# Split weights in the delta rule's own tiles, and no GpSimd splits at stage ends, in a two-block fp32 transformer

## The chip, the cores and the metric

The kernel runs on one core of one Trainium2 chip. The metric is the device time of one execution in microseconds (us). The engines are TensorE (PE in the profile; PEld is its weight load), VectorE (DVE), ScalarE (ACT), GpSimd (POOL) and SyncE (SP), which issues the weight loads. Each engine works through its own list of instructions in the order in which the program was built; what waits in that list holds up all that stands behind it.

## The reference, cut to what matters

One sequence of 256 tokens with 1024 features passes two blocks of two layers each, all in fp32. The first block has differential attention and MLA and then a dense feed-forward (layer 0) or eight experts (layer 1). The change concerns the second block and the ends of some stages. A layer of the second block is, cut down:

```python
for l in range(DEPTH):
    h = rmsnorm(x, norm_mix_g[l])
    proj = h @ w_in[l]                       # all inputs of the mixer, the gates among them
    (qa, ka, va, qd, kd, vd, beta_logit, decay_logit, z, gate_logit) = jnp.split(proj, offsets, axis=-1)
    y_attn = grid_attention(qa, ka, va) @ w_o_attn[l]
    qkv = jax.nn.silu(centred_depthwise_conv(jnp.concatenate([qd, kd, vd], axis=-1), dn_conv_w[l]))
    o = bidir_gated_deltanet(qd, kd, vd, beta, g)      # a chunked linear recurrence, 4 chunks, both directions
    o = rmsnorm(o, dn_out_norm_g[l]) * jax.nn.silu(z)
    y_dn = o @ w_o_dn[l]
    gates = jax.nn.sigmoid(gate_logit).reshape(b, s, N_BRANCH, D_MODEL)
    mixed = gates[:, :, 0] * y_attn + gates[:, :, 1] * y_dn
    x = x + mixed @ w_out[l]
    x = x + ffn(rmsnorm(x, norm_ffn_g[l]))             # w_up, a convolution of width 3, silu, w_down
```

The gates need only `h`, neither the attention nor the delta rule; they can be computed at any time before `mixed`.

## The kernel before

**Weights.** Every weight is read once. The program lists all loads of the whole kernel as numbered jobs of up to 1 MB (128 partitions x 2048 values) and cuts each job into two pieces, called subs here, also numbered through. SP loads a job into one of `RAW` = 2 raw buffers (`_dma`). `_split` (L141) then makes two halves of a sub: `wh`, a rounded copy made by ACT (L152), and `wl`, the rest, made by a subtraction (L154) on DVE or on GpSimd. A matrix product takes three matmuls, high by high, high by low and low by high (L177 to L179 where tokens are the stationary side, `mm3`; L367 to L369 where the weights are, `feat_group`). In the second block there are `HALF` = 3 pairs of buffers for `wh` and `wl`, taken in turn by the sub's number, so the fourth sub waits until the matmuls of the first are done, and a raw buffer is free for the next load when both of its subs are split.

**Which engine subtracts.** DVE, save for two rules: `s.share` = 2 from the start of a mixer of block two to its last gate group gives every second sub to GpSimd, and `s.turn` with `TURN` = 4, set in `tok_parts` (L294 on) where a stage's last product is written out tile by tile, gives the first four subs of the next stage to GpSimd.

**Order.** The code is written in the order of the mathematics; a scheduler then places each engine's instructions by a simulated time line. Casts and splits are written under a priority that moves them ahead (`PRIO`), as far as their buffers allow. So the position of a weight's matmuls in PE's list depends on when its split can be made in that time line.

**The second block's mixer** (`mix2`, L1190) projects the inputs, runs the grid attention (L1342 to L1367) and the delta rule (`delta`, L1396), a generator that is advanced between the projections. The delta rule first inverts a triangular matrix for each chunk on DVE (L1577 to L1615, 1666 to 1676) and then runs 16 steps `pair` (four chunks n = 0 to 3, four pairs of heads), a chain between PE, DVE and ACT (L1690 to L1751); it uses the tiles `kd`, `qk` and `xv` up to its end. Its output is summed in `O` (L1749 to L1751), on GpSimd for n = 0 to 2 and on DVE for n = 3. After the delta rule the code has `dn_out`, then the gates `m` and `G8` (eight groups, two subs each, that is subs 932 to 947 in layer 0 and 1056 to 1071 in layer 1), then the attention's output projection (four subs), the delta rule's (four), and `w_out` (`out_proj`, eight):

```python
for dst in (m, G8):                     # L1267: the gates
    for g in range(4):
        ps = s.fps()
        with s.behind(s.pv if dst is G8 and g >= 3 else None):
            s.feat_group(ps, xh, xl)
        nc.scalar.activation(dst[:, 2 * g:2 * g + 2], ps, AF.Tanh, scale=0.5)
```

**Stage ends.** At the end of a stage each of the two token tiles passes a short serial chain: the residual (L675), the square sum on ACT (L1119), an inverse root of 128x1 values on DVE (L199 to L202, in block one L655 on), the scaling (L1129, in block one L659 to L667), four or eight PE transposes (L214) and their split into halves (L209, L210). PE has no other work in that time. There are seven such ends that `TURN` touches or that lie beside it; the text calls six of them A (mixer, layer 0, block one), B (dense feed-forward), C (mixer, layer 1, block one), D (mixer, layer 0, block two), E (feed-forward, layer 0, block two) and F (mixer, layer 1, block two).

Of the kernel before, what the change touches and what calls it, by code (L numbers as in the profile page):

```python
# [12 lines left out]
F32R = mybir.dt.float32r  # L13
# [11 lines left out]
ALPHA = math.sqrt(2.0)  # L25
# [7 lines left out]
class Net:  # L33
    def __init__(s, ctx, tc, A):
        s.tc, s.nc, s.A = tc, tc.nc, A
        s.const = ctx.enter_context(tc.tile_pool(name="const", bufs=1))
        s.wa = ctx.enter_context(tc.tile_pool(name="wa", bufs=1))
        s.pm = ctx.enter_context(tc.tile_pool(name="psum", bufs=1, space=bass.MemoryType.PSUM))
        s.sc = ctx.enter_context(tc.tile_pool(name="sc", bufs=2))
        s.n_ps = 0  # L40
        s.wx = (0, 0)
        s.share, s.turn = 0, -9
        s.st, s.hs = [None, None], [None, None]
        s.epi = []
        s.pace = None
        s.jobs = []
        s.subs, s.subj = [], []
        s.edge_j = s.edge_i = s.n_ring = 0
        s.am, s.n_view = None, {}
        s.first_j, s.held = 1 << 30, {}  # L50
        s.n_dma = s.n_split = s.n_used = s.n_raw = 0

# [18 lines left out]
    # ---------------------------------------------------------------- weights  # L71
# [3 lines left out]
    TURN = 4  # L75
# [35 lines left out]
    def more(s, j):  # L111
        """Memory of another use that a job around the start of the experts can have, or the empty string."""
        i = j - s.first_j
        if i < 0 or j >= s.edge_j - 12:
            return ""
        while i >= len(s.MORE):
            i -= s.CYC
        return s.MORE[i]

    def _dma(s, j, c):  # L120
        """Loads job j unless its memory may still be held by a job after c."""
        ap, k, n = s.jobs[j]
        tag = s.more(j)
        if tag:
            key, bufs, pool = tag, 1, s.const if tag in ("OA", "Wc", "xTh", "xTl") else s.reg
        elif j >= s.edge_j or s.n_ring % (s.RAW + s.wx[0]) < s.RAW:
            key, bufs, pool, tag = "wa", s.RAW, s.wa, "raw"
        else:
            key, bufs, pool, tag = "wb", s.wx[0], s.wb, "raw"
        use = s.held.setdefault(key, [])  # L130
        if len(use) >= bufs and use[-bufs] > c or j > c + s.AHEAD[c >= s.first_j + 4]:
            return False
        use.append(j)
        s.n_ring += tag == "raw"
        raw = pool.tile([128, 2048], F32, tag=tag, name="raw", bufs=bufs)
        v = raw[:, :k * n].rearrange("p (k n) -> p k n", k=k)
        s.nc.sync.dma_start(v, ap)
        s.jobs[j] = v
        return True

    def _split(s, i):  # L141
        k0, k, n0, n = s.subs[i]
        raw = s.jobs[s.subj[i]][:, k0:k0 + k, n0:n0 + n]
        r = []
        for tag in ("wh", "wl"):
            if i >= s.edge_i or i % (s.HALF + s.wx[1]) < s.HALF:
                w = s.wa.tile([128, 1024], F32R, tag=tag, name=tag, bufs=s.HALF)
            else:
                w = s.wb.tile([128, 1024], F32R, tag=tag, name=tag, bufs=s.wx[1])
            r.append(w[:, :k * n].rearrange("p (k n) -> p k n", k=k))  # L150
        with s.tc.high_priority(offset=s.PRIO):
            s.nc.scalar.copy(r[0], raw)  # L152
            eng = s.nc.gpsimd if 0 <= i - s.turn < s.TURN or s.share and i % s.share == 0 else s.nc.vector
            x = eng.tensor_tensor(out=r[1], in0=raw, in1=r[0].bitcast(F32), op=OP.subtract)  # L154
            if eng is s.nc.gpsimd:
                s.psub = x
        s.subs[i] = (r[0], r[1], k, n)

    def fill(s, ahead):
        last = min(s.n_used, len(s.subs) - 1)  # L160
        while s.n_dma < len(s.jobs) and s._dma(s.n_dma, s.subj[last]):
            s.n_dma += 1
        ahead = min(s.n_used + ahead, max(s.n_used + s.HALF, s.edge_i), len(s.subs))
        while s.n_split < ahead and s.subj[s.n_split] < s.n_dma:
            s._split(s.n_split)
            s.n_split += 1

    def w(s):
        s.fill(s.HALF + s.wx[1])
        r = s.subs[s.n_used]  # L170
        s.subs[s.n_used] = None
        s.n_used += 1
        return r
# [7 lines left out]
    # ---------------------------------------------------------------- helpers  # L181
# [12 lines left out]
    def rsqrt1(s, v, k):  # L194
        """1 / sqrt(-2 v) for one value a row."""
# [36 lines left out]
    def view(s, tag, *shape):  # L232
        """Scratch of 2 KB, two in turn for m0 and three for a0; in the first region it is cut from one tile."""
# [19 lines left out]
    # ---------------------------------------------------------------- T5 bias  # L253
# [54 lines left out]
    # ---------------------------------------------------------------- projections  # L308
    def tok_parts(s, n, K, xch, lead=0, tail=0, tags=("mm", "mm")):
        """Yields (tt, b, psum tile) as each block b of 512 columns of a token tile of x @ w is done  # L310
        (K row blocks, n columns)."""
# [17 lines left out]
        i = 0  # L329
        if tail:  # L330
            s.turn, k = s.n_used, 0
            while k < K:
                u = s.subs[s.turn]
                k += u[1] if len(u) == 4 and isinstance(u[1], int) else u[2]
                s.turn += 1
# [50 lines left out]
    # ---------------------------------------------------------------- block 1 mixer  # L386
# [95 lines left out]
    def mixer1(s, i):  # L482
# [13 lines left out]
        # cq | ckv | kr  # L496
# [146 lines left out]
    def layernorm(s, tt, n, gb, done=None):  # L643
        """Takes half n of token tile tt of x / ALPHA; the second half completes the tile."""
# [38 lines left out]
    # ---------------------------------------------------------------- block 1 feed-forward  # L683
# [302 lines left out]
    # ---------------------------------------------------------------- attention  # L986
# [123 lines left out]
    # ---------------------------------------------------------------- block 2  # L1110
    def rms_h(s, tt, n, gain):
        """Takes half n of token tile tt; the second half completes the tile."""
# [77 lines left out]
    def mix2(s, l):  # L1190
        nc, A = s.nc, s.A
        s.share = s.SHARE
# [41 lines left out]
        # grid attention  # L1234
# [29 lines left out]
        next(dn, None)  # L1264
        OD = s.dn_out(gzh)
# [30 lines left out]
    def grid_qk(s, tt, w, hg, r, qaT, kaT):  # L1296
        """Queries (heads in the order column, group) and keys: gain, rotation, transposes. The queries'
        norm factors are left to the softmax."""
# [94 lines left out]
    # ---------------------------------------------------------------- gated delta rule  # L1393
    def delta(s, l, cT, zb, sv, hg):
# [6 lines left out]
        # decay and beta  # L1401
# [62 lines left out]
        # token layout of q, k, v with l2 norms, and the transposes of q, k  # L1464
# [30 lines left out]
        # decays between the tokens of a chunk; the triangle in use is picked later  # L1495
# [86 lines left out]
        # the last level in strips of four columns or rows, without the zeros of the triangles  # L1582
# [183 lines left out]
    # ---------------------------------------------------------------- block 2 feed-forward  # L1766
# [132 lines left out]
```

## Time and profile before

| | |
|---|---|
| median of 3 runs | 2842.46 us |
| the three runs | 2840.43 to 2845.5 us |
| span of the profiled execution | 2840.1 us |
| PE busy | 2671.5 us, 94% of the span |
| DVE busy | 2195.1 us, 77% |
| ACT busy | 1724.0 us, 61% |
| POOL busy | 511.4 us, 18% |
| splits on DVE (L154) | 1031 |
| splits on POOL (L154) | 123 |

The profile is one execution. Busy time is the time in which an instruction of the engine ran; a PE share of 94% is an average over stages with different limits, and the second block's delta rule and the stage ends are the places where PE is not the limit. In a row of the time line the bracket at its end gives the idle time before the instruction and what ended it.

### The profile page before, as it was taken

To read this page: it belongs to the slowest core of one execution; us is meant where nothing else is said; L and a number is where in the kernel's file an instruction comes from. 1 tells how busy PE (TensorE), PEld (TensorE's weight loads), DVE (VectorE), ACT (ScalarE), POOL (GpSimd) and SP (SyncE) were. 2 spreads that over 40 slices of the span, in tenths; PEclk is the share of its full clock that TensorE was granted. 3 is DMA by queue.
4 is the path that set the end of the run, shared out by engine and by line. 5 is a ranking of instruction groups with operands and counts; after the bars stand their busy time and mean duration, and the time that the engine had idled before them with its cause. 6 is when DMAs were issued, how large, how long until landed. Compare 5 with 4: busy or idle time off the path is not lost. (4 is left out here: it accounts for less than half of the span.)

```text
span 2840.1 us, 42537 instructions
## 1 busy us (share of the span) xinstructions
PE 2671.5 (94%) x16177; PEld 2330.1 (82%) x16177; DVE 2195.1 (77%) x3347; ACT 1724.0 (61%) x2643; POOL 511.4 (18%) x427
## 2 busy tenths in 40 slices
PE   8999999899999999999999999798999999799899
PEld 7988998798887878778787777577778977788897
DVE  6576654646788989889988898789777858987784
ACT  5464543456467777787777777555645535564553
POOL 3235000132400000000000000166520006651100
PEclk9999999999999999999999999898899999899999
DMA  7336555544679999999999998543144544223454
GB/s 216 119 119 197 181 180 170 157 138 137 231 255 359 351 349 357 348 351 344 364 347 352 343 355 293 185 132 91 51 135 159 188 152 135 78 64 121 148 180 161
DMA packets 350097, 610.39 MB, mean 215 GB/s; under 512 B 13626, under 2 KB 175752, under 8 KB 349888
## 3 DMA queue, kind: packets, MB, share of 16 engines
q1 hardware_dynamic: 347120, 601.34, 61.8%
q0 software_dynamic: 2768, 6.28, 0.9%
q8 instruction: 129, 2.11, 0.3%
q14 instruction: 80, 0.66, 0.1%
HBM read 606.56 MB, written 1.05 MB: 214 GB/s over the span
## 5 line engine op out<-in xcount | busy, mean ns | idle before, releaser
L152 ACT CAST wh<-raw 128x1024 fp32r<-128x1024 f32 (+3 forms) x1154 | 1186.8, 1038 | 712.3 <-PE mm L368 188.4
L154 DVE TENSOR_TENSOR wl<-raw,wh 128x1024 fp32r<-128x1024 f32 (+3 forms) x1031 | 1246.3, 1226 | 406.1 <-ACT wh L152 386.2
L367 PE MATMUL mm<-xTh,wh 128*128 128x256 f32 x1632 | 473.9, 290 | 5.3 <-DVE cT L1169 2.9
L369 PE MATMUL mm<-xTh,wl 128*128 128x256 f32 x1632 | 473.7, 290 | 3.5 <-DVE wl L154 1.7
L368 PE MATMUL mm<-xTl,wh 128*128 128x256 f32 x1632 | 471.3, 289 | 0.0
L154 POOL TENSOR_TENSOR wl<-raw,wh 128x1024 fp32r<-128x1024 f32 (+3 forms) x123 | 292.8, 2385 | 916.5 <-ACT wh L152 876.7
L178 PE MATMUL mm<-wl,xg 128*128 128x512 f32 x896 | 356.5, 398 | 1.6
L177 PE MATMUL mm<-wh,xg 128*128 128x512 f32 x896 | 352.6, 395 | 0.0
L179 PE MATMUL mm<-wh,xg 128*128 128x512 f32 x896 | 352.3, 393 | 0.0
L367 PEld LDWEIGHTS mm<-xTh,wh 128*128 128x128 f32 x1632 | 318.8, 195 | 11.3 <-DVE cT L1169 3.7
L369 PEld LDWEIGHTS mm<-xTh,wl 128*128 128x128 f32 x1632 | 318.5, 195 | 7.5 <-POOL wl L154 2.4
L368 PEld LDWEIGHTS mm<-xTl,wh 128*128 128x128 f32 x1632 | 318.3, 195 | 1.1 <-issue 0.2
L178 PEld LDWEIGHTS mm<-wl,xg 128*128 128x128 f32 x896 | 168.3, 188 | 42.8 <-DVE wl L154 7.6
L177 PEld LDWEIGHTS mm<-wh,xg 128*128 128x128 f32 x896 | 168.6, 188 | 37.7
L179 PEld LDWEIGHTS mm<-wh,xg 128*128 128x128 f32 x896 | 168.4, 188 | 36.3
L178 PE MATMUL sd<-wl,ac 128*128 128x512 f32 x448 | 176.3, 393 | 0.0
L179 PE MATMUL sd<-wh,ac 128*128 128x512 f32 x448 | 175.5, 392 | 0.0
L639 POOL DMA_DIRECT2D gb<-in_ln_ffn_g_dram x2 | 1.1, 560 | 966.1 <-DMA raw<-in_expert_w_dram 965.8
L177 PE MATMUL sd<-wh,ac 128*128 128x512 f32 x448 | 144.2, 395 | 0.0
L367 PE MATMUL ex<-xTh,wh 128*128 128x256 f32 x384 | 113.6, 296 | 4.7 <-DVE cT L1169 4.7
L369 PE MATMUL ex<-xTh,wl 128*128 128x256 f32 x384 | 112.6, 293 | 1.5 <-POOL wl L154 1.5
L368 PE MATMUL ex<-xTl,wh 128*128 128x256 f32 x384 | 112.4, 293 | 0.0
(581 smaller groups left out, 4949.4 us busy)
## 6 DMA issues: line engine op xcount, KB each, us to landing
raw<-in_expert_w_dram SPq DMA_DIRECT2D x336, 1024.0 KB, 5.7
raw<-in_w_in_dram SPq DMA_DIRECT2D x74, 1024.0 KB, 5.2
raw<-in_w_up_dram SPq DMA_DIRECT2D x44, 1024.0 KB, 5.1
raw<-in_dense_w_dram SPq DMA_DIRECT2D x33, 1024.0 KB, 5.3
raw<-in_w_down_dram SPq DMA_DIRECT2D x22, 1024.0 KB, 4.9
raw<-in_w_out_dram SPq DMA_DIRECT2D x16, 1024.0 KB, 5.0
raw<-in_w_branch_diff_dram SPq DMA_DIRECT2D x8, 1024.0 KB, 5.1
raw<-in_w_ple_gate_dram SPq DMA_DIRECT2D x8, 1024.0 KB, 5.1
```

Source lines behind the costliest of these rows:

```text
L152: s.nc.scalar.copy(r[0], raw)
L154: x = eng.tensor_tensor(out=r[1], in0=raw, in1=r[0].bitcast(F32), op=OP.subtract)
L177: mm(out, lhsT=lh, rhs=rh, start=start, stop=False)
L178: mm(out, lhsT=lh, rhs=rl, start=False, stop=False)
L179: return mm(out, lhsT=ll, rhs=rh, start=False, stop=stop)
L367: mm(o, lhsT=h[:, kk, sl], rhs=xh[:, kk, :], start=kk == 0, stop=False)
L368: mm(o, lhsT=h[:, kk, sl], rhs=xl[:, kk, :], start=False, stop=False)
L369: mm(o, lhsT=l[:, kk, sl], rhs=xh[:, kk, :], start=False, stop=kk == k - 1)
L639: s.nc.gpsimd.dma_start(gb[:, 0], row_bc(s.A[nm + "_g"], i * D, D))
```

## The change

`TURN` goes: no split is given to GpSimd at a stage's end. Buffers for split weights are no longer taken by the sub's number; `_slot` looks for one that is free in program order, first among the three, then among the tiles in `s.ext`. `s.ext` is set to the delta rule's tiles `kd`, `qk` and `xv` right after the generator has ended in the code, ahead of the gates, and emptied at the start of the next mixer of block two. Each of these tiles holds one split sub (both halves). 46 subs of each layer use one. The numbers of matmuls, casts and loads stay the same; 20 of the subtractions move from GpSimd to DVE on balance. Cut to its core:

```diff
+    def _slot(s, i):
+        some = [("wa", s.HALF)]
+        if s.wx[1] and i < s.edge_i:
+            some.append(("wb", s.wx[1]))
+        for key, bufs in some + [(t, 1) for t in s.ext]:
+            use = s.busy.setdefault(key, [])
+            if len(use) < bufs or use[-bufs] < s.n_used:
+                use.append(i)
+                return key
+
-    def _split(s, i):
+    def _split(s, i, slot):
...
+        if slot in ("wa", "wb"):
+            pool, bufs = (s.wa, s.HALF) if slot == "wa" else (s.wb, s.wx[1])
+            ws = [pool.tile([128, 1024], F32R, tag=tag, name=tag, bufs=bufs) for tag in ("wh", "wl")]
+        elif slot == "xv":
+            ws = [s.reg.tile([128, 1024], F32R, tag=slot, name="ww", bufs=2) for _ in range(2)]
+        else:
+            w = (s.const if slot in ("OA", "Wc") else s.reg).tile([128, 2, 1024], F32R, tag=slot, name="ww")
+            ws = [w[:, 0], w[:, 1]]
...
-            eng = s.nc.gpsimd if 0 <= i - s.turn < s.TURN or s.share and i % s.share == 0 else s.nc.vector
+            eng = s.nc.gpsimd if s.share and i % s.share == 0 else s.nc.vector
...
-        ahead = min(s.n_used + ahead, max(s.n_used + s.HALF, s.edge_i), len(s.subs))
-        while s.n_split < ahead and s.subj[s.n_split] < s.n_dma:
-            s._split(s.n_split)
+        while ahead and s.n_split < len(s.subs) and s.subj[s.n_split] < s.n_dma:
+            slot = s._slot(s.n_split)
+            if slot is None:
+                break
+            s._split(s.n_split, slot)
             s.n_split += 1
...
-        if tail:
-            s.turn, k = s.n_used, 0
-            while k < K:
-                u = s.subs[s.turn]
-                k += u[1] if len(u) == 4 and isinstance(u[1], int) else u[2]
-                s.turn += 1
...
     def mix2(s, l):
-        s.share = s.SHARE
+        s.share, s.ext = s.SHARE, ()
...
         next(dn, None)
+        s.ext = ("kd", "qk", "xv")
         OD = s.dn_out(gzh)
```

What this does to the engines' lists is shown at three places. Line numbers behind the change are 11 to 15 higher.

**ACT in layer 0's delta rule and grid attention.** Before, the casts of gate weights (`wh`) stand between the rows of the convolution (`cT`, `th`), of the attention (`e`, `eT`), of the delta rule (`cv`, `j`) and the gates' own evictions (`m`):

```order
795 L152 CAST wh<-raw 128x1024
796 L1473 COPY cv<-sd 128x512 x2
797 L1227 ACTIVATE th<-cT 128x512
798 L1479 ACTIVATE j<-cv 128x512 x2
799 L1359 COPY eT<-at 128x512
800 L152 CAST wh<-raw 128x1024
801 L1273 ACTIVATE m<-ex 128x512
802 L1163 ACTIVATE cT<-mm,cw 128x256
803 L152 CAST wh<-raw 128x1024
804 L1351 ACTIVATE e,gsum<-at,gnm,gr 128x256 x2
805 L152 CAST wh<-raw 128x1024
806 L1273 ACTIVATE m<-mm 128x512
```

After, the same stretch of ACT's list:

```order
790 L1363 ACTIVATE e,gsum<-at,gnm,gr 128x256 x2
791 L1485 COPY cv<-sd 128x512 x2
792 L1238 ACTIVATE th<-cT 128x512
793 L1491 ACTIVATE j<-cv 128x512 x2
794 L1371 COPY eT<-at 128x512
795 L1174 ACTIVATE cT<-mm,cw 128x256
796 L1285 ACTIVATE m<-ex 128x512
797 L1363 ACTIVATE e,gsum<-at,gnm,gr 128x256 x2
798 L1371 COPY eT<-at 128x512
799 L1238 ACTIVATE th<-cT 128x512
800 L1363 ACTIVATE e,gsum<-at,gnm,gr 128x256 x2
801 L1371 COPY eT<-at 128x512
```

The casts of gate weights from sub 935 on have left this stretch: before, 14 casts stand in rows 795 to 851; after, none stands between row 786 and the delta rule's first chunks.

**POOL at the delta rule's end and the end of layer 0's mixer.** Before, `u` and `O` are the delta rule's output sums, the rows with `wl` are the splits, and `Sa` and `X` are the clearing of the next layer's tiles:

```order
157 L1751 TENSOR_TENSOR O<-u,O 64x128 x2
158 L1745 TENSOR_TENSOR u<-u 128x128
159 L1751 TENSOR_TENSOR O<-u,O 64x128 x2
160 L390 DMA m_20527<-in_ffn_conv_w_dram 88x128
161 L390 DMA m_20532<-in_ffn_conv_w_dram 44x128
162 L1683 MEMSET Sa 128x1024
163 L154 TENSOR_TENSOR wl<-raw,wh 128x1024 x2
164 L1550 MEMSET X 128x1024
165 L154 TENSOR_TENSOR wl<-raw,wh 128x1024 x3
166 L390 DMA m_22487<-in_dn_conv_w_dram 60x128
167 L154 TENSOR_TENSOR wl<-raw,wh 128x1024
```

After:

```order
150 L1763 TENSOR_TENSOR O<-u,O 64x128 x2
151 L401 DMA m_20525<-in_ffn_conv_w_dram 88x128
152 L401 DMA m_20530<-in_ffn_conv_w_dram 44x128
153 L169 TENSOR_TENSOR wl<-raw,wh 128x1024
154 L1695 MEMSET Sa 128x1024
155 L169 TENSOR_TENSOR wl<-raw,wh 128x1024
156 L169 TENSOR_TENSOR ww<-raw,ww 128x1024 x2
157 L169 TENSOR_TENSOR wl<-raw,wh 128x1024 x2
158 L169 TENSOR_TENSOR ww<-raw,ww 128x1024
159 L169 TENSOR_TENSOR wl<-raw,wh 128x1024 x2
160 L1562 MEMSET X 128x1024
161 L401 DMA m_22463<-in_dn_conv_w_dram 60x128
```

The splits of the gate weights on POOL now stand behind the last output sums of chunk n = 2 (the first of them, row 153, is that of sub 938), and the three splits between `X` and the next load at the stage's end are gone.

**DVE at the end of layer 0's mixer (end D).** `r_y`, `r_t` and `r2v` are the inverse root's 128x1 values, `h` is the scaled tile that PE transposes next. Before:

```order
1668 L675 SCALAR_TENSOR_TENSOR xt<-ex,xt 128x512
1669 L1124 SCALAR_TENSOR_TENSOR r2v<-r_20379 128x1
1670 L199 TENSOR_SCALAR r_y<-r2v 128x1
1671 L201 TENSOR_SCALAR r_t<-r_y,r2v 128x1
1672 L202 SCALAR_TENSOR_TENSOR r_y<-r_t,r_y 128x1
1673 L1553 MEMSET X 128x32
1674 L201 TENSOR_SCALAR r_t<-r_y,r2v 128x1
1675 L202 SCALAR_TENSOR_TENSOR r_y<-r_t,r_y 128x1
1676 L201 TENSOR_SCALAR r_t<-r_y,r2v 128x1
1677 L202 SCALAR_TENSOR_TENSOR r_y<-r_t,r_y 128x1
1678 L1129 SCALAR_TENSOR_TENSOR h<-xt,r_y,g 128x512 x2
1679 L675 SCALAR_TENSOR_TENSOR xt<-mm,xt 128x512
```

After:

```order
1681 L169 TENSOR_TENSOR ww<-raw,ww 128x1024
1682 L219 SCALAR_TENSOR_TENSOR r_y<-r_t,r_y 128x1
1683 L686 SCALAR_TENSOR_TENSOR xt<-mm,xt 128x512
1684 L218 TENSOR_SCALAR r_t<-r_y,r2v 128x1
1685 L169 TENSOR_TENSOR wl<-raw,wh 128x1024
1686 L219 SCALAR_TENSOR_TENSOR r_y<-r_t,r_y 128x1
1687 L169 TENSOR_TENSOR ww<-raw,ww 128x1024
1688 L218 TENSOR_SCALAR r_t<-r_y,r2v 128x1
1689 L1135 SCALAR_TENSOR_TENSOR r2v<-r_20389 128x1
1690 L219 SCALAR_TENSOR_TENSOR r_y<-r_t,r_y 128x1
1691 L216 TENSOR_SCALAR r_y<-r2v 128x1
1692 L1140 SCALAR_TENSOR_TENSOR h<-xt,r_y,g 128x512 x2
```

Three splits now stand inside the first tile's chain on DVE, and the second tile's residual and the start of its root stand ahead of the first tile's scaling.

## Rows read from the trace of the kernel before

**Rows 1.** Waits of PE: releaser, us in total, times, longest.
```profile
PE sd L214 <- DVE h L1129: 39.7, 6, 18.2
PE mm L177 <- DVE xt L675: 11.4, 2, 5.7
```

**Rows 2.** All engines in layer 0's delta rule: start:end, length; PE, PEld, DVE, ACT, POOL; clock.
```profile
1960.00:2020.00 60.00, 53.71 (x366) 48.86 (x366) 57.22 (x94) 35.81 (x77) 30.71 (x26) 0.86 0.26 80
```

**Rows 3.** Matmuls of line 368 alone by stretch: PE busy (count), PEld busy (count), clock.
```profile
1960.00:2040.00 80.00, 26.82 (x87) 18.23 (x87) 0.83 0.24 74
...
2460.00:2540.00 80.00, 27.16 (x87) 18.57 (x87) 0.83 0.24 74
```

**Rows 4.** Time line of layer 0: GpSimd's last output sum, the gates' last matmul, two later matmuls.
```profile
2067.85 1.02 POOL L1751 TENSOR_TENSOR O<-u,O 64x128 f32<-64x128 f32 x2
...
2077.38 0.28 PE L369 MATMUL mm<-xTh,wl 128*128 128x256 f32 x1
...
2094.73 0.28 PE L368 MATMUL ex<-odT,wh 128*128 128x256 f32 x1
...
2096.13 0.28 PE L369 MATMUL mm<-odT,wl 128*128 128x256 f32 x1
```

**Rows 5.** The page's weight loads (count, KB, us to landing); splits on DVE (busy, mean ns).
```profile
raw<-in_w_in_dram SPq DMA_DIRECT2D x74, 1024.0 KB, 5.2
...
L154 DVE TENSOR_TENSOR wl<-raw,wh 128x1024 fp32r<-128x1024 f32 x1004 | 1227.0, 1239 | 375.5 <-ACT wh L152 355.6 <-DMA raw<-in_expert_w_dram 2.6 <-PE ex L1023 2.1
```

**Rows 6.** Time line of layer 1: GpSimd's last output sum and the gates' last matmul.
```profile
2567.48 1.09 POOL L1751 TENSOR_TENSOR O<-u,O 64x128 f32<-64x128 f32 x2
...
2577.61 0.28 PE L369 MATMUL mm<-xTh,wl 128*128 128x256 f32 x1
```

**Rows 7.** Splits (line 154) by stretch: DVE busy (count), POOL busy (count), clock.
```profile
1960.00:2040.00 80.00, 7.62 (x6) 17.91 (x7) 0.83 0.24 74
...
2460.00:2540.00 80.00, 9.15 (x6) 14.66 (x6) 0.83 0.24 74
```

**Rows 8.** DVE's time line in layer 0's delta rule: long instructions beside usual ones.
```profile
1960.02 4.16 DVE L1577 TENSOR_TENSOR XP<-X,XP 128x512 f32<-128x512 f32 x2
...
1978.97 1.13 DVE L1603 TENSOR_TENSOR XP<-Mb,X 128x512 f32<-128x512 f32 x1
...
1980.74 2.25 DVE L191 SCALAR_TENSOR_TENSOR rs_y<-rs_t,rs_y 128x16 f32<-128x16 f32 x1
...
1984.71 0.17 DVE L191 SCALAR_TENSOR_TENSOR rs_y<-rs_t,rs_y 128x16 f32<-128x16 f32 x1
...
1989.05 2.50 DVE L1603 TENSOR_TENSOR XP<-X,XP 128x512 f32<-128x512 f32 x1
```

**Rows 9.** PE's time line there: the same four transposes, twice.
```profile
1949.56 0.60 PE L214 MATMUL at<-ident,e 128*128 128x128 f32 x4
...
1965.43 1.24 PE L214 MATMUL at<-ident,e 128*128 128x128 f32 x4 [2.92 <-ACT e L1351]
```

**Rows 10.** Time line of end D on three engines.
```profile
2125.71 6.98 POOL L154 TENSOR_TENSOR wl<-raw,wh 128x1024 fp32r<-128x1024 f32 x3 [0.25 <-DVE X L1553]
2125.81 2.30 DVE L202 SCALAR_TENSOR_TENSOR r_y<-r_t,r_y 128x1 f32<-128x1 f32 x1
...
2128.45 1.96 DVE L202 SCALAR_TENSOR_TENSOR r_y<-r_t,r_y 128x1 f32<-128x1 f32 x1
2130.45 3.46 DVE L1129 SCALAR_TENSOR_TENSOR h<-xt,r_y,g 128x512 f32<-128x512 f32 x2
2133.30 1.97 PE L214 MATMUL sd<-ident,h 128*128 128x128 f32 x8 [6.05 <-DVE h L1129]
...
2137.35 0.16 DVE L202 SCALAR_TENSOR_TENSOR r_y<-r_t,r_y 128x1 f32<-128x1 f32 x1
...
2138.05 1.41 DVE L1129 SCALAR_TENSOR_TENSOR h<-xt,r_y,g 128x512 f32<-128x512 f32 x2
2138.85 1.54 PE L214 MATMUL sd<-ident,h 128*128 128x128 f32 x6 [3.59 <-DVE h L1129]
```

More of the change, by code (lines that the diff above doesn't have):

```diff
@@ L41, in __init__ @@
         s.wx = (0, 0)
-        s.share, s.turn = 0, -9
+        s.share = 0
         s.st, s.hs = [None, None], [None, None]
@@ L51, in __init__ @@
         s.n_dma = s.n_split = s.n_used = s.n_raw = 0
+        s.busy, s.ext = {}, ()
     @contextmanager
@@ L74 @@
     SHARE = 2
-    TURN = 4
     PRIO = 3000
@@ L144, in _split @@
         r = []
[L145 to L149, printed above, removed]
+        if slot in ("wa", "wb"):
[6 more added lines that the diff above has]
+            ws = [w[:, 0], w[:, 1]]
+        for w in ws:
             r.append(w[:, :k * n].rearrange("p (k n) -> p k n", k=k))
@@ L162, in fill, with w @@
             s.n_dma += 1
-        ahead = min(s.n_used + ahead, max(s.n_used + s.HALF, s.edge_i), len(s.subs))
-        while s.n_split < ahead and s.subj[s.n_split] < s.n_dma:
-            s._split(s.n_split)
-            s.n_split += 1
[L168 to L173, printed above, removed]
+        while ahead and s.n_split < len(s.subs) and s.subj[s.n_split] < s.n_dma:
[3 more added lines that the diff above has]
+            s._split(s.n_split, slot)
+            s.n_split += 1
+    def w(s, n=1):
+        s.fill(1)
+        r = s.subs[s.n_used:s.n_used + n]
+        s.subs[s.n_used:s.n_used + n] = [None] * n
+        s.n_used += n
+        return r if n > 1 else r[0]
     def mm3(s, out, lh, ll, rh, rl, start, stop):
```

## The prediction

> **What bounds the kernel now.** I read the waits of PE first, since PE is busy for 94% of the span: what PE waits for is what a change off PE can win. The longest group is the scaled tile of the stage ends in block two, 39.7 us in six waits, and the residual at the ends of block one's mixers is another, 11.4 us in two [rows 1]. Then I read the stretches. In layer 0's delta rule DVE is busy for 57.22 of 60 us [rows 2], so DVE sets the pace there, and PE is nevertheless busy for 53.71, because the scheduler puts the gates' matmuls into the delta rule's shade. How much of PE's work that is, is seen from line 368 alone, which each sub runs eight times: 87 matmuls between 1960 and 2040 us, that is eleven subs, and in layer 1 the same 87 [rows 3]. The second place to see is the last matmul of the gates, at 2077.38 and at 2577.61 us [rows 4, 6]: behind it PE runs on almost without a break to the end of the mixer, so a delay of this instruction is a delay of the kernel.
>
> The change touches two things that hardly meet: where the gates' weights are split (per layer), and what stands beside the serial chains at the stage ends.
>
> **Part 1: the gates leave the delta rule.** Subs 935, 936 and 937 are given the tiles `kd`, `qk` and `xv`. These are in use until the delta rule's last steps, so the splits can't be made earlier, and since there are two raw buffers of two subs each, the loads of 938 and all that follow wait for them. ACT's order shows it: no cast of a gate weight is left in the stretch where the kernel before has them one after another. PE's order agrees: behind sub 934 come only the attention's and the delta rule's rows, and 935 stands among those of the last chunk. The buffers meant to give more room thus take it away until the delta rule ends.
>
> What it costs, in the times of the trace before and then less what the delta rule gains. One sub: twelve steps from 2094.73 to 2096.13 us are 1.40 us, 0.117 us a matmul [rows 4], 24 of them 2.8 us. In POOL's order the split of sub 938 stands behind the last output sum of chunk n = 2, which ended at 2068.87 us [rows 4]. A split there takes 17.91 / 7 = 2.56 us [rows 7], so it is done at 2071.4. Then PE has twelve subs (936 to 947) before the gates end, 12 x 2.81 = 33.7 us, and one wait: 940 can be loaded only into the raw buffer that 938 leaves, 5.2 us [rows 5], then come a cast, which I estimate at 1 us by the split of 1.24 us on DVE [rows 5] that writes as much, and a split on POOL of 2.56, so it is ready at 2080.2, while PE has done 938 and 939 at 2077.0; 3.2 us. The gates end at 2071.4 + 33.7 + 3.2 = 2108.3 instead of 2077.5 us: 30.8 us later. In layer 1, by the same order with its own rows, 2568.57 + 2.56 + 33.7 + 3.2 = 2608.0 instead of 2577.7 [rows 6]: 30.3 us. Together 61.1. The bounds: 6.4 less if the loads come early enough, and a load's landing of 5.2 more in each layer if ACT, whose casts of 938 and 939 stand ahead of copies of the delta rule's last steps, holds these up.
>
> What the delta rule gains. DVE loses its own splits there, 7.62 us in layer 0 and 9.15 in layer 1 [rows 7]. It also loses waits beside GpSimd's splits: a product of two that took 4.16 us against 1.13 each, a root step of 2.25 against 0.17, a product of 2.50 against 1.13 [rows 8], together 1.90 + 2.08 + 1.37 = 5.4 us; I take the same for layer 1. The gain is 13.0 and 14.5, together 27.5 us, since DVE is the bound in nearly all of that stretch. Less than that is possible where the chain is bound by PE and ACT (from 2020 us on), and more if every split on GpSimd cost DVE its whole length (rival 1). Net of part 1: 61.1 - 27.5 = 33.6 us slower.
>
> The clock speaks against a full gain. The granted clock over the first 60 us is 0.86 [rows 2], a mixture of the two levels of 1.2 and 2.4 GHz, and it is there, after PE had waited 2.92 us, that four transposes take 1.24 us instead of 0.60 [rows 9]. With the gates gone PE waits far more often. The Trainium skill (TensorE: Matmul & The Clock Gate, Part 1, "What's actually happening") says that the slow clock is the default and activity is what releases it. The trace's rows agree as far as they go. By that rule alone the delta rule's own matmuls would run at the lower level for most of it, which is rival 2; the sum here goes by the rows and takes no such loss.
>
> **Part 2: the stage ends.** Here the change does what it says. At end D three splits run on GpSimd for 6.98 us, and beside them two steps on 128x1 values take 2.30 and 1.96 us instead of 0.16, and the scaling 3.46 instead of 1.41 [rows 10]: 2.14 + 1.80 + 2.05 = 6.0 us, nearly the whole of PE's wait of 6.05. This goes. But three splits now stand in that chain on DVE, 3 x 1.24 = 3.7 us [rows 5], which leaves 2.3. The second tile's wait of 3.59 us [rows 10] falls too, since its residual and root are now done ahead of the first tile's scaling; what must remain is one scaling and a transpose, so I take 2.5. Together 5 us at D, and 5 at F, whose lists read alike. At A and C PE waits 5.7 us each [rows 1] and two splits enter DVE's chain; from D's rows the stall is at most 6.0 and the splits cost 2.5, so 0 to 4, taken as 2 each. At E the rows of D bound it the same way, 0 to 3, taken as 2, since DVE's chain was mostly done when GpSimd began. B I take at 0: the splits there are short and its chain waits on the last tile's product. Sum 16 us faster, 9 to 21 by these bounds (D and F at 2.3 each and the others near half; D and F at 6 each).
>
> More buffers behind the delta rule I cost at nothing: PE runs there without waits of weight in the rows, so the new buffers win nothing but an earlier split at D and F, which is counted.
>
> **The sum.** 2840.1 (the profiled span) + 33.6 - 16 = 2857.7 us. The runs lie 2.4 us above the span (2842.46 against 2840.1), so 2860.1: **2860 us**, with a range of its own from 2849 (the stage ends at 21 and no wait for 940 in either layer) to 2870 (the ends at 9 and a part of one further landing).
>
> **Rivals.**
> *1. GpSimd's splits held DVE up for their whole length (faster).* The relief in the delta rule is then all the split time of both engines: 7.62 + 17.91 and 9.15 + 14.66, together 49.3 us [rows 7], and the stage ends come out at the upper 21. The time is 2842.5 + 61.1 - 49.3 - 21 = 2833 us. It decides from a relief of 61.1 - 21 + 5.7 = 45.8 us in the two layers. For it speaks that the three instructions of rows 8 lost most of a split's length; against it that these make 5.4 of 17.9 us. The Trainium skill has a rule that would make it so: the two engines' shared port is held for a whole instruction, and the other engine blocks (SBUF — State Buffer, "SBUF: two separate sides"). The trace agrees for the 128x1 steps of rows 10; whether all of GpSimd's time in the delta rule costs DVE its own, no row shows.
> *2. The delta rule gets no quicker where it counts (slower still).* PE's own matmuls in the chain take the lower clock, 0.64 us more for four [rows 9], in some ten visits a layer 6.4 us of the relief, and the raw buffers cost a further landing of 5.2 [rows 5]: 61.1 + 10.4 - (27.5 - 12.8) - 16 = 40.8, time 2883 us. For it speaks the wait ahead of the slow transposes; against it that DVE, not PE, is the bound up to 2020 us.
> *3. The two cancel.* A relief of 21 us a layer, half way to rival 1, gives 61.1 - 42 - 16 = 3.1, 2846 us.
>
> **How the numbers follow.** A measurement of this kernel can tell about 0.2%, 5.7 us, from no change, that is 2836.8 to 2848.1 us. Forecast 0.47, rival 1 0.20, rival 2 0.20, rival 3 0.13. Faster is rival 1, 0.20; same is rival 3, 0.13; slower is the forecast and rival 2, 0.67. The range goes from just above rival 1's time to just above rival 2's, 2834 to 2886 us; it leaves out about half of rival 1 and the far end of rival 2.
>
> **What would show it.** In the changed profile: line 379 (the former 368) with few or no matmuls between the delta rule's start and its last 20 us, DVE's splits there gone, and the stretch from the delta rule's first product to its last chunk shorter by some 13 us; the gates' last matmul some 17 us later than before, counted from the mixer's start, in each layer; PE's waits at D and F of some 4 and 1 us instead of 6.05 and 3.59. The forecast is wrong if the delta rule shortens by more than 20 us a layer, or if the gates' matmuls still run inside it. If PE's granted clock falls to near one half in the delta rule and the relief is under 8 us, rival 2 is right.

## The result, and the profile after

The changed kernel takes 2878.01 us (median of four runs, 2877.27 to 2884.94) against 2841.99 us of the kernel before (four runs): a ratio of 1.0133 with a 95% interval of 1.0121 to 1.0145. That is 36 us slower where 17.5 were forecast. The sign and the place were right, the size was half: 2878 lies between the forecast's 2860 and the second rival's 2883. The profiled execution spans 2876.0 us.

PE's work is the same, but it waits in other places. The page's busy times, and the longest waits of PE (releaser, us in total, times, longest), which answer to [rows 1]:

```profile
PE 2690.7 (94%) x16177; PEld 2348.6 (82%) x16177; DVE 2192.4 (76%) x3367; ACT 1724.9 (60%) x2643; POOL 468.9 (16%) x407
```

```profile
PE sd L231 <- DVE h L1140: 41.1, 6, 19.0
PE at L231 <- ACT e L1363: 13.6, 6, 3.7
PE sd L231 <- DVE cv L1499: 11.8, 3, 6.2
PE sd L231 <- DVE O L1398: 7.9, 2, 4.1
```

The wait for the scaled tile `h`, which the change was to shorten, was 39.7 us [rows 1] and is 41.1. The wait for block one's residual (11.4 us in two) is off the list's head, and the wait for `O`, the delta rule's output, has risen to 7.9 us. Before, it was 2.4 (L231 is the former L214: some lines moved by 17, not by 11 to 15):

```profile
PE sd L214 <- DVE O L1386: 2.4, 2, 1.6
```

**Inside the delta rule.** Layer 0's first 60 us on all engines (answers to [rows 2]), then line 379 alone (the former 368, answers to [rows 3]) and line 169 alone (the former 154, answers to [rows 7]), both over the 74 us up to the first chunk:

```profile
1954.00:2014.00 60.00, 45.44 (x187) 38.05 (x187) 50.19 (x115) 33.77 (x93) 22.13 (x25) 0.54 0.00 1
```

```profile
1943.00:2017.00 74.00, 3.34 (x11) 2.36 (x10) 0.58 0.00 1
```

```profile
1943.00:2017.00 74.00, 0.00 (x0) 0.00 (x0) 0.58 0.00 1
```

Eleven matmuls of line 379 where there were 87 (in 80 us), no split at all, no load (1 GB/s), and a granted clock of 0.54 where it was 0.86: the gates have left, as the order had shown. The two layers, cut at four marks that every kernel has (first transposes of the mixer's input `h`; first product with `xv`, that is the delta rule's first chunk; first product with `oaT`, right behind the gates; last product with `mT`, the end of `w_out`; then the second tile's transposes of `h` at end D or F), all in us:

| stretch | before | after | difference | forecast |
|---|---|---|---|---|
| layer 0, input to first chunk | 204.8 | 188.5 | -16.3 | -13.0 |
| layer 0, first chunk to the gates' end | 39.0 | 85.0 | +46.0 | +30.8 |
| layer 0, gates' end to the end of `w_out` | 49.7 | 45.8 | -4.0 | 0 |
| end D | 11.6 | 11.4 | -0.2 | -5 |
| layer 1, input to first chunk | 207.1 | 192.1 | -14.9 | -14.5 |
| layer 1, first chunk to the gates' end | 37.2 | 79.6 | +42.5 | +30.3 |
| layer 1, gates' end to the end of `w_out` | 53.8 | 46.3 | -7.5 | 0 |
| end F | 11.6 | 10.8 | -0.8 | -5 |

The rest is block one (up to the first mark, 1833.7 us before and 1829.1 after, -4.6) and the two feed-forwards (-1.1 and -3.1). The sum is +35.9 us, the difference of the spans.

**Behind the delta rule** the time line of layer 0 shows why the second row is so long (rows of five engines, in order of time; start and length in us, idle time and its releaser in brackets):

```profile
2046.18 1.05 ACT L167 CAST ww<-raw 128x1024 fp32r<-128x1024 f32 x1
...
2048.66 36.46 SPq L137 DMA_DIRECT2D raw<-in_w_in_dram  x5
...
2049.54 1.11 POOL L1763 TENSOR_TENSOR O<-u,O 64x128 f32<-64x128 f32 x2
...
2054.06 1.99 ACT L167 CAST wh<-raw 128x1024 fp32r<-128x1024 f32 x2 [0.46 <-DMA raw<-in_w_in_dram]
...
2055.24 2.36 POOL L169 TENSOR_TENSOR wl<-raw,wh 128x1024 fp32r<-128x1024 f32 x1 [2.37 <-ACT wh L167]
...
2057.66 0.51 PE L380 MATMUL ex<-xTh,wl 128*128 128x256 f32 x1 [0.82 <-POOL wl L169]
...
2058.18 0.41 PE L379 MATMUL ex<-xTl,wh 128*128 128x256 f32 x1
...
2060.10 0.41 PE L379 MATMUL ex<-xTl,wh 128*128 128x256 f32 x1
...
2076.25 2.44 DVE L206 TENSOR_TENSOR rs_t<-rs_y 128x8 f32<-128x8 f32 x2
2076.28 2.39 POOL L169 TENSOR_TENSOR ww<-raw,ww 128x1024 fp32r<-128x1024 f32 x1 [5.19 <-ACT ww L167]
...
2078.61 2.39 DVE L207 SCALAR_TENSOR_TENSOR rs_t<-rs_t,oss 128x8 f32<-128x8 f32 x2
2078.63 2.35 POOL L169 TENSOR_TENSOR wl<-raw,wh 128x1024 fp32r<-128x1024 f32 x1
...
2081.86 1.11 PE L231 MATMUL sd<-ident,O 128*128 128x128 f32 x4 [4.07 <-DVE O L1398]
...
2102.61 0.28 PE L378 MATMUL mm<-oaT,ww 128*128 128x256 f32 x1
```

From top to bottom: the cast of sub 935 into one of the tiles is done only at 2047.2 us; only then a raw buffer is free and the load of 938 and 939 goes out, 2048.66; it lands at 2054.06; the split on POOL ends at 2057.6, seven us behind POOL's last output sum (2050.65) where the forecast had 2.56; the gate matmuls behind it run at 0.21 us a step (nine steps from 2058.18 to 2060.10 us) instead of 0.117, with a granted clock of 0.52 there (1.00 from 2062.5 us on); and in the middle of the gates PE waits 4.07 us for `O`, because two pairs of steps of its norm take 2.44 and 2.39 us on DVE (0.24 a pair otherwise), exactly beside two splits on POOL. The gates end at 2102.6 us, before at 2077.5 [rows 4].

**End D**, to compare with the last group of rows ahead of the prediction [rows 10]:

```profile
2146.70 1.05 ACT L167 CAST wh<-raw 128x1024 fp32r<-128x1024 f32 x1 [2.08 <-DMA raw<-in_w_up_dram]
...
2147.66 0.63 ACT L1130 ACTIVATE h<-xt 128x512 f32<-128x512 f32 x1
...
2149.54 1.19 DVE L169 TENSOR_TENSOR ww<-raw,ww 128x1024 fp32r<-128x1024 f32 x1
...
2151.78 1.22 DVE L169 TENSOR_TENSOR wl<-raw,wh 128x1024 fp32r<-128x1024 f32 x1 [0.20 <-ACT wh L167]
...
2152.99 1.22 DVE L169 TENSOR_TENSOR ww<-raw,ww 128x1024 fp32r<-128x1024 f32 x1
...
2155.43 1.97 PE L231 MATMUL sd<-ident,h 128*128 128x128 f32 x8 [7.06 <-DVE h L1140]
...
2159.78 1.97 PE L231 MATMUL sd<-ident,h 128*128 128x128 f32 x8 [2.38 <-DVE h L1140]
```

GpSimd no longer stands beside the chain, but PE's first wait is 7.06 us, longer than the 6.05 before: besides the three splits that the order showed, a cast for the next stage stands ahead of the square sum (L1130) on ACT and waits 2.08 us for its load.

### The profile page after: what moved, and what is told of

Read it like the earlier page. It is cut to its first block, busy times and chain, and to the rows that moved or that the text cites. A ratio compares the mean times of both kernels' runs of the same rounds, so it can differ in the third digit from the quotient of the medians.

```text
span 2876.0 us, 42477 instructions
## 1 busy us (share of the span) xinstructions
PE 2690.7 (94%) x16177; PEld 2348.6 (82%) x16177; DVE 2192.4 (76%) x3367; ACT 1724.9 (60%) x2643; POOL 468.9 (16%) x407
## 3 DMA queue, kind: packets, MB, share of 16 engines
q1 hardware_dynamic: 347120, 601.34, 61.1%
## 5 line engine op out<-in xcount | busy, mean ns | idle before, releaser
L167 ACT CAST wh<-raw 128x1024 fp32r<-128x1024 f32 (+3 forms) x1062 | 1092.1, 1039 | 633.3 <-PE mm L196 175.6
L169 DVE TENSOR_TENSOR wl<-raw,wh 128x1024 fp32r<-128x1024 f32 (+3 forms) x965 | 1164.6, 1225 | 376.9 <-ACT wh L167 355.4
L378 PE MATMUL mm<-xTh,wh 128*128 128x256 f32 x1320 | 382.9, 290 | 10.2 <-DVE cT L1180 7.4
L380 PE MATMUL mm<-xTh,wl 128*128 128x256 f32 x1320 | 381.8, 289 | 1.8 <-DVE wl L169 1.0
L379 PE MATMUL mm<-xTl,wh 128*128 128x256 f32 x1320 | 380.6, 288 | 0.0
L169 POOL TENSOR_TENSOR wl<-raw,wh 128x1024 fp32r<-128x1024 f32 (+1 forms) x97 | 235.7, 2430 | 649.2 <-ACT wh L167 600.0
L380 PEld LDWEIGHTS mm<-xTh,wl 128*128 128x128 f32 x1320 | 256.5, 194 | 3.7 <-DVE wl L169 1.4
L169 DVE TENSOR_TENSOR ww<-raw,ww 128x1024 fp32r<-128x1024 f32 (+1 forms) x86 | 107.7, 1252 | 54.9 <-ACT ww L167 49.8
L167 ACT CAST ww<-raw 128x1024 fp32r<-128x1024 f32 (+1 forms) x92 | 94.7, 1033 | 90.1 <-PE mm L380 31.0
L194 PE MATMUL mm<-wh,xTh 128*128 128x512 f32 (+4 forms) x278 | 102.7, 376 | 4.0 <-ACT wh L167 2.9
```

The costliest lines, as they stand in the source:

```text
L194: mm(out, lhsT=lh, rhs=rh, start=start, stop=False)
L378: mm(o, lhsT=h[:, kk, sl], rhs=xh[:, kk, :], start=kk == 0, stop=False)
L379: mm(o, lhsT=h[:, kk, sl], rhs=xl[:, kk, :], start=False, stop=False)
L380: mm(o, lhsT=l[:, kk, sl], rhs=xh[:, kk, :], start=False, stop=kk == k - 1)
```

## The experiments

All ratios are against the kernel before on the same chip. First the two halves of the change alone, then six kernels that place the gates, or make their splits, in another way.

### Only the stage ends: turn_only

```diff
-        s.ext = ("kd", "qk", "xv")
```

> The changed kernel without the line that hands out the delta rule's tiles: three buffers for split weights throughout, and no splits on GpSimd at stage ends. Theory A (the loss of the change comes from the gates leaving the delta rule, the stage ends are a separate small gain): the gates are back inside the delta rule, and what is left of the changed trace is its gain of some 6 us in block one and 0 to 5 at the ends of block two, so 2829 to 2837 us. Theory B (the splits moved to DVE's chains at the stage ends are themselves a loss of several us each): 2848 us or more. PE's wait at end D: A expects 5 to 7 us in the first tile, B over 7.

Measured: 2827.14 us, 0.9945 (0.9928 to 0.9962), 16 us faster than the kernel before. That is theory A's case, though 2 us below its range. PE's time line at end D and its last split on DVE ahead of it:

```profile
2124.91 1.22 DVE L169 TENSOR_TENSOR wl<-raw,wh 128x1024 fp32r<-128x1024 f32 x1
...
2127.35 1.97 PE L231 MATMUL sd<-ident,h 128*128 128x128 f32 x8 [4.02 <-DVE h L1140]
...
2131.38 0.90 PE L231 MATMUL sd<-ident,h 128*128 128x128 f32 x3 [2.06 <-DVE h L1140]
```

With three splits in the chain on DVE PE waits 4.02 and 2.06 us instead of 6.05 and 3.59; the first is less than the 5 to 7 us that theory A expected. By the marks of the table, block one gains 4.1 us, D 3.6 and F 3.5, and the stretch over end E and layer 1's delta rule 3.3. So the second half of the change is a gain, and theory B is out. The gain at D and F repeats: 7.9 to 8.1 us in all four kernels without the tiles, 11.6 before. That of block one is partly scatter: the eight kernels without the rule for GpSimd reach the first mark at 1826.6 to 1831.7 us, and six_only, which has the rule, at 1830.4.

### Only the six buffers: six_only

```diff
-            eng = s.nc.gpsimd if s.share and i % s.share == 0 else s.nc.vector
+            eng = s.nc.gpsimd if 0 <= i - s.turn < s.TURN or s.share and i % s.share == 0 else s.nc.vector
...
+        if tail:
+            s.turn, k = s.n_used, 0
```

> The changed kernel with the rule for GpSimd at stage ends put back (the first four subs of the next stage are split there), so six buffers alone are left of the change. Theory A: the whole loss of part 1 stays, and the gain in block one goes, so 2882 to 2890 us, with the gates' last matmul as late as in the changed kernel. Theory B: 2842 to 2860 us.

Measured: 2887.84 us, 1.0160 (1.0139 to 1.0182). The buffers alone cost 45 us. By the marks of the table, the way to the first chunk is 14.3 and 12.7 us shorter than before, and the way from there to the gates' end 45.9 and 40.9 us longer. The two halves are not quite independent: without the tiles the stage ends are worth 16 us, with them 9.8 (2887.84 - 2878.01). The rule for GpSimd still matters beside the tiles, since D and F take 14.0 and 13.6 us here and 11.4 and 10.8 in the changed kernel. It is the buffers that take the gain back: with them alone D and F are 2.4 and 2.0 us longer than before.

### The tiles handed out later: late_dn

```diff
-        s.ext = ("kd", "qk", "xv")
         OD = s.dn_out(gzh)
...
         mT = []
         s.share = 0
+        s.ext = ("kd", "qk", "xv")
```

> The changed kernel with one line moved: the delta rule's tiles are handed out behind the gates and the attention's output projection, just ahead of the delta rule's output projection. Theory A: the gates run inside the delta rule as in the kernel before, and six buffers serve the rest of the mixer and the next feed-forward, 2828 to 2838 us. A rival to it (more buffers for the feed-forward cost something themselves, because casts that wait for loads stand ahead of the square sums on ACT at ends D and F): slower than the kernel with no such tiles by 2 to 6 us.

Measured: 2826.55 us, 0.9947 (0.9926 to 0.9968): as fast as turn_only, 1.5 us below theory A's range, and faster than both kernels of the case. The gates end 39.8 and 40.1 us behind the first chunk, near the 39.0 and 37.2 of before. The loss is gone with one line moved by a few lines, so it is the place in the program at which the tiles enter, not their use, that costs 50 us. The rival is half right: in its trace PE waits at D for 5.75 and 2.25 us where turn_only has 4.02 and 2.06, and what six buffers win elsewhere (3.7 and 4.1 us in the two feed-forwards) pays for that. At F nothing is lost (8.2 us against 8.1).

```profile
2126.14 1.97 PE L231 MATMUL sd<-ident,h 128*128 128x128 f32 x8 [5.75 <-DVE h L1140]
...
2130.36 0.90 PE L231 MATMUL sd<-ident,h 128*128 128x128 f32 x3 [2.25 <-DVE h L1140]
```

### No splits on GpSimd behind the delta rule: dve_gates

```diff
         s.ext = ("kd", "qk", "xv")
+        s.share = 0
```

> The changed kernel with every split behind the delta rule on DVE, none of them on GpSimd (the sharing is ended where the tiles are handed out). It asks what made the gates end 25 us late in layer 0 where 12 were forecast. Theory C (GpSimd: the first gate's split stands behind the delta rule's output sums there, and two steps of the output norm take 2.4 us each beside GpSimd's splits, which holds up PE's transposes of O): 4 to 8 us a layer less, 2862 to 2870 us. Theory D (the loads: each pair of subs waits for a raw buffer that the pair before leaves, one load after the other): 2874 to 2880 us.

Measured: 2856.03 us, 1.0054 (1.0038 to 1.0070): 22 us less than the changed kernel, more than theory C asked for. The stretch from the first chunk to the gates' end falls from 85.0 to 73.4 us in layer 0 and from 79.6 to 71.6 in layer 1. The steps of the output norm and the transposes of `O` (to compare with 2.44, 2.39 and 4.07 us in the changed kernel):

```profile
2072.60 0.24 DVE L206 TENSOR_TENSOR rs_t<-rs_y 128x8 f32<-128x8 f32 x2
2072.80 0.24 DVE L207 SCALAR_TENSOR_TENSOR rs_t<-rs_t,oss 128x8 f32<-128x8 f32 x2
...
2076.12 0.60 PE L231 MATMUL sd<-ident,O 128*128 128x128 f32 x4
```

So of 51 us between turn_only and the changed kernel (2878.01 - 2827.14), 22 are GpSimd's. Theory D can at most explain the other 29.

### The gates behind the delta rule without the tiles: gates_behind and behind_dve

Here the second half of the change stays, no tile is handed out, and the last six gate groups are placed behind the delta rule by hand. In behind_dve GpSimd makes none of the splits from the gates on.

```diff
-                with s.behind(s.pv if dst is G8 and g >= 3 else None):
+                with s.behind(s.pv if dst is G8 or g >= 2 else None):
```

> Three buffers and no tiles handed out, as in the run turn_only (2827 us), but the last six of the eight gate groups are placed behind the delta rule's last product with xv, so that their matmuls leave the shade as in the changed kernel while four of their subs are cast ahead of it and the raw buffers behind these are already loaded. If the loss is PE work out of the shade alone: the price is that of the changed kernel without its late loads, 12 to 15 us a layer over turn_only, 2851 to 2858 us. If waits behind it (loads one after the other, GpSimd, the transposes of O in the gates' midst) are most of it and need the tiles: 2835 to 2845 us. If they come with the place and not with the tiles: 2865 us or more, near the changed kernel.

> The kernel of gates_behind with every split from the gates on made on DVE. The difference to gates_behind is what GpSimd's splits cost when the gates stand behind the delta rule (5 to 10 us a layer expected from the 22 us that the same edit gave the changed kernel); the difference to dve_gates (2856 us) is what handing out the tiles costs beyond that, by loads that start late: 4 to 7 us a layer, so 2842 to 2848 us. If the late loads cost nothing: 2854 to 2858 us.

Measured: gates_behind 2873.30 us, 1.0115 (1.0097 to 1.0132); behind_dve 2852.94 us, 1.0043 (1.0026 to 1.0060). The first is the expectation's third case: moving the gates alone, with no tile handed out, costs 46 of the 51 us. The second misses its range on the side where the late loads cost little: 3.1 us (2856.03 - 2852.94) for both layers, not 8 to 14, and the intervals of the two ratios overlap, so it is not clear of nothing. One way to split the 51 us:

| | us | runs |
|---|---|---|
| the gates out of the delta rule's shade, their splits moved to DVE | 25.8 | behind_dve - turn_only |
| loads that start late because of the tiles | 3.1 | dve_gates - behind_dve |
| splits on GpSimd with the gates in that place | 22.0 | after - dve_gates |

The first entry is not the price of the place alone, since two things change in it. Of the kernels with the gates inside, turn_dve (below) too has their splits on DVE, and against it the place costs 13.0 us (2852.94 - 2839.97). With GpSimd's share in both it costs 46.2 (2873.30 - 2827.14). So which engine makes the gates' splits decides most of what it costs to have the gates behind the delta rule.

The third entry is not one mechanism. In the pair with the tiles it lies behind the first chunk (11.6 and 8.0 us). In the pair without them (20.4 us) it lies mostly ahead of it: from the input to the first chunk gates_behind takes 197.8 and 198.9 us, behind_dve 190.3 and 192.8, and behind the first chunk, to the gates' end, they differ by 1.0 and 1.7 us. Layer 0's way from the input to the first chunk, all engines and then the splits alone (DVE, POOL), first in gates_behind and then in behind_dve:

```profile
1827.80:2025.56 197.76, 160.81 (x925) 140.57 (x925) 170.08 (x342) 108.05 (x235) 108.51 (x105) 0.78 0.25 76
1827.80:2025.56 197.76, 17.72 (x15) 35.42 (x15) 0.78 0.25 76
```

```profile
1827.70:2018.02 190.32, 156.50 (x925) 137.16 (x925) 166.46 (x346) 108.46 (x236) 101.44 (x102) 0.80 0.26 79
1827.70:2018.02 190.32, 21.65 (x18) 28.16 (x12) 0.80 0.26 79
```

Three splits fewer on GpSimd, 7.3 us, leave DVE 7.6 us less to do outside its splits (170.08 - 17.72 against 166.46 - 21.65); in layer 1 it is 6.2 us for 7.3. So in this place they hold DVE up for nearly their whole length. Since three more splits on DVE take 3.9 us of that back, the rest of the 7.5 us by which the way is shorter was not isolated.

### The transposes of O behind the gates: o_last

```diff
-                s.tr(pt[:, c], o[:, 2 * c:2 * c + 2].rearrange("p h d -> p (h d)"))
+                with s.behind(s.fg):
+                    s.tr(pt[:, c], o[:, 2 * c:2 * c + 2].rearrange("p h d -> p (h d)"))
```

(`s.fg` is the last matmul of the gates, and the call of `dn_out` stands behind them.)

> The changed kernel with the eight transposes of O placed behind the last matmul of the gates, the rest as it is. In the changed trace PE stood 4.1 us for O between two gate subs and lost 7.9 us there in all, in layer 0. If that is a loss of its own: 5 to 7 us a layer less, 2863 to 2868 us. If PE only waits elsewhere instead (for the loads): 2873 us or more.

Measured: 2871.62 us, 1.0109 (1.0092 to 1.0126). It takes 6.4 us off, 3.2 a layer: half of what the gap seemed to offer, though more than nothing. In layer 0's gates PE no longer waits 4.1 us for `O`; it waits 1.3 us for ACT's eviction `m` and 1.1 for two splits instead.

### What a split on GpSimd costs DVE inside the delta rule: turn_dve

```diff
 (turn_only)
+        s.share = 0
         OD = s.dn_out(gzh)
```

> The kernel turn_only (2827 us) with every split from the gates on made on DVE, the gates inside the delta rule. It asks what a split on GpSimd costs DVE there. By the long instructions counted in the trace of before, 5.4 us for seven splits, against 1.24 us for each split on DVE: 2 to 4 us a layer slower, 2831 to 2835 us. If a split on GpSimd holds DVE up for its whole 2.5 us (the first rival of the prediction): 6 to 9 us a layer faster, 2809 to 2815 us.

Measured: 2839.97 us, 0.9997 (0.9988 to 1.0007), 12.8 us slower than turn_only, twice what I expected and the opposite of the prediction's first rival. The splits of the same 60 us, first in turn_only and then in turn_dve (DVE busy, POOL busy, clock):

```profile
1951.00:2011.00 60.00, 6.26 (x5) 13.56 (x5) 0.85 0.29 88
```

```profile
1951.00:2011.00 60.00, 15.46 (x12) 0.00 (x0) 0.96 0.34 105
```

DVE has 9.2 us more of splits in that stretch, and the way from the input to the first chunk becomes 0.9 us longer in layer 0 and 4.7 in layer 1; most of the rest lies further on (9.0 us between the gates' end and the end of `w_out`, both layers, where PE waits 4.4 and 4.5 us for `O` instead of 0.7 and 1.6). Layer 0's way to the first chunk, all engines and then the splits alone, first in turn_only and then in turn_dve:

```profile
1829.60:2033.33 203.73, 176.78 (x1164) 159.16 (x1164) 178.02 (x347) 120.77 (x250) 123.62 (x110) 0.89 0.32 97
1829.60:2033.33 203.73, 23.97 (x20) 49.19 (x20) 0.89 0.32 97
```

```profile
1831.70:2036.34 204.64, 179.02 (x1166) 161.59 (x1166) 179.54 (x356) 120.94 (x251) 102.46 (x102) 0.87 0.32 97
1831.70:2036.34 204.64, 34.93 (x28) 28.28 (x12) 0.87 0.32 97
```

Eight splits move. DVE's splits take 11.0 us more, and its other work takes 9.4 us less (178.02 - 23.97 against 179.54 - 34.93); in layer 1, with seven splits, 11.2 more and 8.5 less. So the 20.9 and 17.2 us of splits on GpSimd held DVE up for about half their length here, which is less than the same splits take on DVE.

## Why the prediction was wrong

**The direction and the cause were right.** The gates left the delta rule, as the order on ACT and PE had shown, and that is what made the kernel slower. late_dn shows it from the other side: with the gates back inside it is 1.8% faster than the changed kernel.

**The relief was right.** Forecast 13.0 and 14.5 us, measured 16.3 and 14.9 ahead of the first chunk. six_only, where the stage ends are as before, has 14.3 and 12.7, together 27.0 against 27.5; of the 14.9 in layer 1 a part belongs to end E. In the changed kernel the low clock (0.54 of the full one, near the lower of the two levels) left no less than was forecast, so the step of rival 2 that subtracts 6.4 us a layer did not show, though the clock did fall; what the relief would be at the higher clock no run shows. That it would fall is what the Trainium skill says (TensorE: Matmul & The Clock Gate, Part 1, "What's actually happening"), and the trace agrees: 0.86 with the gates inside, 0.54 without.

**The step that failed is the gates' delay**, 61.1 us in the sum and 88.5 in the trace. Its parts in layer 0, where 30.8 became 46.0: the chunk phase itself was held up (POOL's last output sum comes 33.1 us behind the first chunk's product, before 30.4: +2.7); the split of 938 came 7.0 us behind that sum instead of 2.56, because the load had only just landed (+4.4); some twenty of its matmuls ran at 0.21 us instead of 0.117 (+1.9); PE's wait behind 939 was 1.5 us instead of 3.2 (-1.7); and in the gates' midst the transposes of `O` took PE from 2077.8 to 2085.7 us, 7.9 us in which twelve gate matmuls, 1.4 us, were done (+6.5). Together 13.8 of the 15.2 us. These are times that lie one behind the other in the trace, not what each is worth: with the transposes moved away (o_last) the stretch is 3.0 us shorter, not 6.5. The load's further landing stood in the prediction as a bound and in rival 2, so I had the mechanism and gave it no weight. The transposes I had not seen at all, though the order of PE shows them between two gate subs. dve_gates tells what they have in common: with the splits on DVE the same stretch is 34.4 us longer than before in each layer, 68.8 together, close to the 61.1 of the forecast. GpSimd's part was priced as a split of 2.56 us at two places of a layer; it is 22 us of the kernel.

**Against it, waits vanished that I had not counted.** From the gates' end to the end of `w_out` the changed kernel is 4.0 and 7.5 us quicker, since `O` and its transposes are now done earlier than they are asked for: in layer 0 PE's waits there fall from 2.6 to 0.4 us, and the eight transposes are already counted in the stretch before.

**The stage ends.** The term of 16 us is what turn_only measures (16.0 of the medians, 13.9 of the spans), though its parts fell out otherwise: D and F give 7.1 there, not 10. In the changed kernel itself it was 9.8 us: block one gave 4.6 us (4 were forecast, and part of the 4.6 is scatter), but D and F gave 0.2 and 0.8 instead of 5 each. The step that failed is "more buffers behind the delta rule I cost at nothing". With six of them, a fourth split and casts that wait for their loads get in front of the chain, on DVE and ahead of ACT's square sum; without them D and F gave 3.6 and 3.5, and six_only has the buffers' part alone, a loss of 2.4 and 2.0. The bounds of this term, 9 and 21, do not follow from its parts either: with D and F at 6 each and the others at their upper ends it is 23, with the others as taken 18.

**Put together.** From the forecast's 17.6 us, 27.4 more for the gates' delay and 9.0 more at D and F, less 3.7 of relief and 11.5 behind the gates, come to 38.8; block one and the feed-forwards take off some 3, which leaves the 35.9 of the spans. So the error in the total is smaller than that of its largest term because other terms were wrong the other way, which is luck.

**Rivals.** Rival 1 (faster) falls by the relief itself, 31.2 us for both layers where it asks for 49.3, and by turn_dve: were DVE held up for GpSimd's whole length in the delta rule, moving those splits to DVE would have made it faster, and it became slower. The Trainium skill's rule behind it (SBUF — State Buffer, "SBUF: two separate sides") holds where a DVE step with two inputs meets a split, as the rows of 2.44 and 2.39 us show. It does not follow that all of GpSimd's time is lost: in turn_only about half was, in gates_behind nearly all. Rival 2 had the time nearly right (2883 us) for a reason that was half wrong: the further landing was there, the lost relief was not. Rival 3 did not occur.

## What to carry to other kernels

Memory that becomes free at the end of a long phase is not a further buffer for work that could run inside that phase: given out in program order, it binds the next weights to the phase's end, and with few load buffers all that follow them too. Read from the built order which matmuls the bound engine's shade holds, and whether a new buffer moves any of them out, before counting what the buffer may win; and count the whole queue behind the first late split (its load, the other users of the slow engine, transposes that stand in between), not that split alone. Taking slow helper splits away from a serial chain paid here even where three of them entered the chain on the faster engine.

## What I had not expected of the hardware

A pair of steps of 128x8 values on DVE took 2.44 us instead of 0.24 beside a split on GpSimd, and yet making some eight splits a layer on GpSimd inside the delta rule took less of DVE's time than making them on DVE: 9.4 us against 11.0 in layer 0, 8.5 against 11.2 in layer 1. The whole kernel is 12.8 us faster with them there, 2827.14 against 2839.97 us. With the gates behind the delta rule it is the other way round, 2873.30 against 2852.94. How much a GpSimd operation takes from DVE is not one figure: about half of the splits' length in turn_only, nearly all of it in gates_behind. The single long instruction in a time line is no price for all of them.
